# Hybrid attention block, out projection prepared on another schedule: sums of m later, loads on SP by an account, wo in 256 KB pieces, tail additions reordered

## The chip, the cores and the metric

One core of a Trainium2 chip runs the kernel. Its engines run their own instruction streams beside one another and meet by semaphores: TensorE (PE, matmuls; PEld are its weight loads), VectorE (DVE), ScalarE (ACT), GpSimd (POOL) and SyncE (SP), which here issues nearly all DMA transfers. An engine takes its instructions in order, and so does SP: a transfer that must wait holds up all that is queued behind it. The metric is the device time of one execution in microseconds (us), the median of the runs; 477.0 before the change.

## What is computed

One layer for 1024 tokens of width 1024: projections of x, two attention groups, gates, an out projection, a residual and a layer norm. All of it is float32.

```python
def reference(x, w_in, rel_pos_bias, sink_logits, w_out, ln_gain, ln_bias):
    h = jnp.einsum('bsd,de->bse', x, w_in[layer])
    q_a, k_a, v_a, z_a, q_b, k_b, v_b, z_b = jnp.split(h, SPLIT_POINTS, axis=-1)
    y_a = neighborhood_attention(q_a, k_a, v_a, rel_pos_bias)   # 8 heads of 64, 2-D window
    qb, kb = rotary(q_b, positions), rotary(k_b, positions)
    y_b = windowed_gqa_with_sink(qb, kb, v_b, sink_logits)      # 8 heads, |i - j| <= 128
    mixed = jnp.concatenate([y_a * jax.nn.silu(z_a), y_b * jax.nn.silu(z_b)], axis=-1)
    y = jnp.einsum('bse,ed->bsd', mixed, w_out[layer])
    x = layer_norm(DEEPNORM_ALPHA * x + y, ln_gain[layer], ln_bias[layer])
```

(The reshapes into heads are left out.) This change touches the last two lines and the preparation for them.

## The kernel before

**Number format.** A float32 operand is split into two float16 parts, hi (ACT: a scaled copy) and lo (DVE or POOL: the operand minus hi), and a product is three matmuls, hi by hi, hi by lo and lo by hi. On DVE such a lo is one instruction (L996 for wo, L1085 for m); on POOL it is two for wo (L998 and L999) and one for m.

**The stages.** Up to about 122 us come the projection of V and the first six of 21 projections of x. Then a loop of 138 steps runs 128 attention units, of group b first, then of group a. A unit is 128 queries of one head pair: scores (`stage_qk`, L851 and L852), bias and row maximum on DVE (L861), exp on ACT (L876), the split of the probabilities (ACT L886, DVE L887), a DMA transpose by SP (L890, tile `tr`), and, for four units together, the product with V (`stage_pv`, L916), the division (L925, L928), a transpose on TensorE (L939) and the gate, which writes the tile z of the transposed mixed matrix m (L942, L945). A transpose is used some steps after its unit's scores. Between the units `pump` and `pump_to` hand TensorE matmuls of the other 15 projections (L421) and, at the end, first products of the out projection (`out_head`). After step 137 `final()` does the rest of it.

**The out projection.** Features are grouped into four pairs of tiles of m. For the pairs 0 and 1 (group b) it goes by a scheme with seven products for eight, with sums of quarters: of m, S1 to S4 (A11, A12, A21, A22 are the quarters, cut by tile of the pair and half of the tokens), and of wo, T1 to T4 (B11 to B22 the quarters). The pairs 2 and 3 are multiplied plainly. The products are called q1, q2, q5, q6, q7, q3, p4 and d (the dictionary `TERMS`); several of them gather in one PSUM bank, and between them DVE adds what the bank holds to the output row block xr (`add`, L1181), so that the next product of a bank has to wait for the add ahead of it. For row blocks t and 4 + t the results come from the same products. When a block is whole, DVE takes its statistics (L1187, L1191), and ACT, POOL and SP do the norm and the store.

**What prepares it during the loop.** wo is loaded once to be scanned for a scale (`wo_load` L976, `wo_scan`; `wo_scale` with the small matmul L775), block 1 a second time for the sums T, whose parts go to DRAM (`td`, L1013) and come back at the end as tiles T0 to T3 (`t_soon`, L1030). The other parts of wo come in 14 loads `wob0` to `wob13` of 256 KB (`b_load` L1052), each into a staging buffer that an earlier one's split has freed: `wob5` reuses that of `wob0`, and so on. `b_split` queues a part's hi (L1061) and lo, `m_queue` the sums and splits of m. Row blocks of x are read by `x_soon` (L1040, scaled on ACT L1044) and in `final()` (`x_load` L1173, `x_scale` L1176).

**What sets the order.** Tables of step numbers by hand: SCAN_LD, M_AT, B_LD, B_AT, T_RD and X_RD say in which step an operation is queued. A queue per engine then gives them out: `pop` takes an operation when those it depends on were given out in earlier steps (for SP two or more steps earlier), `fill_in` one that fits into the gap that an account shows (`due`, time booked on an engine by estimated costs, against `at_step`, when a step is expected to begin). An operation of the kind "any" goes to ACT, DVE or POOL, whichever the account gives first. `need` pulls an operation forward when its result is about to be read. All this happens while the program is built; on the chip the order is fixed.

Of the kernel before, what the change touches and what calls it, by code (L numbers as in the profile page):

```python
# [7 lines left out]
F32 = mybir.dt.float32  # L8
# [36 lines left out]
SCAN_LD = [1, 8, 16, 24]  # L45
SCAN = (2, 3, 1, 0)
M_AT = [58, 67, 75, 83, 91, 99, 107]
B_KEYS = [("B11", 0), ("B21", 0), ("B11", 1), ("B21", 1), ("B22", 0), ("B22", 1), ("B11", 2), ("B21", 2),
          ("B11", 3), ("B21", 3), ("B12", 2), ("B22", 2), ("B12", 3), ("B22", 3)]
B_LD = [58, 59, 60, 61, 62, 69, 71, 73, 76, 80, 92, 94, 96, 98]  # L50
B_AT = [68, 70, 72, 74, 78, 80, 89, 91, 93, 95, 110, 112, 114, 116]
# [13 lines left out]
def hybrid_block(ctx, tc, xT, x, wt, wv, wo, bias, sink, gain, lbias, cos, sin, bmask, out):  # L65
# [84 lines left out]
    class Op:  # L150
        def __init__(self, eng, fn, deps, prio, cost=None):
            self.eng, self.fn, self.deps, self.step = eng, fn, [d for d in deps if d is not None], None
            self.cost = cost or WORK.get(eng, 0)
            self.prio, self.born, self.lag, self.fin = prio, clock["step"], 2 if eng == "sp" else 0, 0.0

# [43 lines left out]
    def fill_in(eng):  # L199
        now = at_step(clock["step"])  # L200
        ready = [op for e in (eng, "any") for op in queues[e] if op.prio > 1 and (e == eng or eng in op.cost) and all(
            d.step is not None and d.step + d.lag < clock["step"] + (d.eng == eng) and (d.eng == eng or d.fin < now)
# [761 lines left out]
    SUM, LOW = {"dve": 0.65, "pool": 1.2}, {"dve": 0.65, "pool": 1.85}  # L964
# [6 lines left out]
    wor, scans, t_ops = {}, [], []  # L971

    def wo_load(i, *deps):
        def load():
# [3 lines left out]
        load_ops["wor", i] = enq("sp", load, *deps)  # L978
        load_ops["wor", i].lag = 4

    def wo_scan(i):
        def scan(eng, b):
            m = wom[:, 4 * i + b:4 * i + b + 1]
            if eng == "act":
                nc.scalar.activation(junk2, wor[i][:, b], AF.Abs, accum_out=m)
            else:
                nc.vector.tensor_reduce(m, wor[i][:, b], axis=mybir.AxisListType.X, op=ALU.add,
                                        apply_absolute_value=True)

        for b in range(4):  # L990
            scans.append(enq("any", lambda eng, b=b: scan(eng, b), load_ops["wor", i], prio=1.9,
                             cost={"act": 0.85, "dve": 0.68}))
# [468 lines left out]
```

## Time and profile before

| | us |
|---|---|
| median of three runs (475.72, 477.00, 477.08) | 477.0 |
| the profiled execution | 477.5 |
| its span | 475.6 |
| scores of unit 64 (step 64) begin | 244.32 |
| scores of unit 96 begin | 311.53 |
| scores of unit 127, the last, begin | 378.99 |
| first product of `final()` (q5 of block 0) | 395.51 |
| mean granted clock of TensorE | 0.982 |

How to read the lines that follow below. In the first section of the page each engine has its busy time, its share of the span and its number of instructions. A line of the waits reads: engine, tile and line that waited, what it waited for, then us in total, times, and the longest. A line of the windows has a stretch of the span, its length, busy time and number of instructions of PE, PEld, DVE, ACT and POOL, then the granted clock (1.00 is full speed), the busy share of the DMA engines by packet time (it can pass 1), and GB/s. In a timeline, each row is start, duration, engine, line, operation, tiles out and in, the number of instructions merged, and in brackets the idle time ahead and what ended it. "SPq" is SP's queue: a long row is a transfer whose issue waited. Durations are of one profiled execution.

### The profile page before, as it was taken

The page shows a single profiled execution, that of the slowest core. Times are in us where ns is not written, and L with a number is a line of the kernel's source. Part 1 is how long each engine was busy: PE and PEld are TensorE (multiplying, and loading weights), DVE is VectorE, ACT ScalarE, POOL GpSimd, SP SyncE. Part 2 cuts the span into 40 slices and gives each one's busy share as a digit, 9 for nine tenths or more (in the row PEclk, how much of TensorE's full clock was granted, in tenths as well). Part 3 has the DMA queues.
Part 4 walks back from the last instruction along what each step waited for, and adds up shares of the span by engine and source line. Part 5 has one row for each costly group of instructions (what it writes and reads, how often), then busy time and mean ns, then how long its engine had stood idle before and what let it go on. Part 6 is the DMA issues. An engine that isn't in the chain of part 4 may idle for free.

```text
span 475.6 us, 9303 instructions
## 1 busy us (share of the span) xinstructions
PE 442.4 (93%) x3205; PEld 253.3 (53%) x3205; DVE 339.0 (71%) x826; ACT 313.6 (66%) x658; POOL 275.8 (58%) x292
## 2 busy tenths in 40 slices
PE   9999999999999999899979999959999969898993
PEld 8997744444455555455545555435555644343443
DVE  6979958069887888886887778775778734556554
ACT  5859689494797897868777777775788733133211
POOL 0300345648477388898287798984986331357551
PEclk9999999999999999999998999998999999999998
DMA  8911779951489995456999779569587698011122
GB/s 283 405 44 50 258 218 285 261 202 42 161 209 172 221 200 110 94 101 96 168 263 211 133 171 173 134 117 224 144 143 183 139 297 335 20 68 68 44 78 78
DMA packets 125791, 78.54 MB, mean 165 GB/s; under 512 B 96944, under 2 KB 106032, under 8 KB 125104
## 3 DMA queue, kind: packets, MB, share of 16 engines
q1 hardware_dynamic: 125600, 77.82, 66.2%
q8 instruction: 25, 0.41, 0.3%
q14 instruction: 22, 0.18, 0.1%
q10 hardware_dynamic: 144, 0.13, 0.1%
HBM read 46.44 MB, written 8.42 MB: 115 GB/s over the span
## 4 chain that ended last, share of the span: by engine, by line
PE 59%; DVE 10%; ACT 9%; issue 9%; DMA 6%; POOL 6%; SPq 0%; DVEq 0%; ACTq 0%; POOLq 0%
PE ps_pj L421 22%; PE ps_s L1146 9%; PE ps_s L528 6%; PE ps_pj L1146 5%; PE ps_t L916 4%; DMA tr<-split 3%; PE ps_pj L528 3%; PE ps_t L528 3%; ACT split L886 3%; PE ps_s L851 2%; PE ps_s L852 2%; PE ps_t L1146 2%; POOL wl L239 2%; DVE split L887 2%; DVE qs L297 2%
## 5 line engine op out<-in xcount | busy, mean ns | idle before, releaser
L421 PE MATMUL ps_pj<-xf,wh 128*128 128x512 f16 x672 | 203.8, 383 | 0.3 <-DVE qs L297 0.3
L421 PE MATMUL ps_pj<-xf,wl 128*128 128x512 f16 x336 | 128.7, 383 | 0.0
L887 DVE SCALAR_TENSOR_TENSOR split<-ps_s,split 128x384 f16<-128x384 f32 (+1 forms) x128 | 66.8, 522 | 44.3 <-ACT split L886 43.1
L421 PEld LDWEIGHTS <-wh 128*128 128x128 f16 x672 | 64.1, 99 | 63.0 <-issue 3.6
L876 ACT ACTIVATE ps_s<-sn,nm 128x385 f32<-128x385 f32 (+3 forms) x128 | 70.8, 553 | 28.8 <-DVE nm L861 28.5
L886 ACT ACTIVATE split<-ps_s 128x384 f16<-128x384 f32 (+1 forms) x128 | 58.3, 456 | 3.0 <-DMA tr<-split 1.3
L238 POOL TENSOR_SCALAR wr<-wr,wsc 128x512 f32<-128x512 f32 x26 | 20.5, 790 | 68.2 <-ACT wh L233 52.7
L421 PEld LDWEIGHTS <-wl 128*128 128x128 f16 x336 | 33.1, 99 | 39.1 <-issue 1.6
L916 PEld LDWEIGHTS <-tr 128*128 128x128 f16 (+1 forms) x1056 | 37.2, 98 | 14.5 <-DMA tr<-split 12.1
L851 PE MATMUL ps_s<-ks,qs 128*128 128x384 f16 (+2 forms) x128 | 40.0, 313 | 4.2 <-DVE split L887 3.4
L861 DVE CUSTOM_DVE_ANT_0 sn<-ps_s,bias,sg 128x368 f32<-128x368 f32 (+1 forms) x64 | 36.3, 567 | 9.1 <-PE ps_s L852 7.8
L861 DVE CUSTOM_DVE_ANT_0 sn<-ps_s,bm,nsk 128x384 f32<-128x384 f32 (+1 forms) x64 | 40.7, 636 | 1.2 <-PE ps_s L852 1.0
L852 PE MATMUL ps_s<-ks,qs 128*128 128x384 f16 (+2 forms) x128 | 40.0, 313 | 0.0
L1146 PEld LDWEIGHTS <-m 128*128 128x128 f16 x234 | 22.4, 99 | 30.6 <-issue 8.2
L239 POOL TENSOR_TENSOR wl<-wr,wh 128x512 f16<-128x512 f32 x26 | 32.7, 1256 | 2.2
L1193 ACT ACTIVATE sd<-mv,eps 128x1 f32<-128x1 f32 x8 | 2.4, 294 | 41.7 <-DVE mv L1191 41.7
L916 PE MATMUL ps_t<-va,tr 128*128 128x65 f16 (+1 forms) x528 | 20.7, 195 | 8.3 <-DMA tr<-split 8.3
L339 POOL COPY ks<-ks 64x512 f16<-64x512 f16 x40 | 26.0, 662 | 3.9 <-DVE ks L299 1.2
L1181 DVE SCALAR_TENSOR_TENSOR xr<-ps_s,yc,xr 128x512 f32<-128x512 f32 (+1 forms) x22 | 15.7, 729 | 15.8 <-PE ps_s L1146 15.8
L1146 PE MATMUL ps_s<-T,m 128*128 128x512 f16 x84 | 20.4, 379 | 5.1 <-DVE xr L1181 5.1
L1085 POOL TENSOR_TENSOR m<-z,m 128x512 f16<-128x512 f32 x15 | 17.1, 1162 | 13.7 <-ACT m L1082 13.6
L1242 POOL TENSOR_TENSOR xr<-xr,gb 128x512 f32<-128x512 f32 x13 | 16.5, 1271 | 13.2 <-ACT xr L1240 8.1
(208 smaller groups left out, 906.1 us busy)
## 6 DMA issues: line engine op xcount, KB each, us to landing
ws<-in_wt SPq DMA_DIRECT2D x15, 512.0 KB, 6.8
wr<-in_wt SPq DMA_DIRECT2D x26, 256.0 KB, 3.9
wor<-in_wo SPq DMA_DIRECT2D x5, 1024.0 KB, 5.7
xr<-in_x SPq DMA_DIRECT2D x8, 512.0 KB, 6.4
out<-xr SPq DMA_DIRECT2D x15, 256.0 KB, 2.0
wob<-in_wo SPq DMA_DIRECT2D x14, 256.0 KB, 4.1
bias<-in_bias SPq DMA_DIRECT2D x8, 440.0 KB, 4.0
wvraw<-in_wv SPq DMA_DIRECT2D x9, 320.0 KB, 5.6
```

The source lines that it names most:

```text
L239: nc.gpsimd.tensor_sub(l, raw, h)
L339: nc.gpsimd.tensor_copy(place(t, o, half, col), place(t, a, half, col))
L421: nc.tensor.matmul(ps, a[:, k % 4, :], mv, start=(k == 0 and i == 0), stop=(k == KT - 1 and i == 2))
L528: nc.tensor.matmul(ps[:, :320], lh[:, ts], rh[:, cs], start=(k == ko[0] and i == 0), stop=(k == ko[-1] and i == 2))
L851: nc.tensor.matmul(ps[:, :n], q, sl[0], start=True, stop=False)
L852: nc.tensor.matmul(ps[:, :n], q, sl[1], start=False, stop=True)
L861: nc.vector.tensor_tensor_reduce(sn[:, :n], ps[:, :n], bias_t, sg[:, c:c + 1], init, op0=ALU.add, op1=ALU.min, accum_out=nm)
L876: nc.scalar.activation(pt[:, :m], sn[:, :m], AF.Exp, bias=nm, scale=-1.0, accum_out=acc)
L886: nc.scalar.activation(hl[:, :m, 0, :], src, AF.Copy, scale=PSCALE)
L887: nc.vector.scalar_tensor_tensor(hl[:, :m, 1, :], src, PSCALE, hl[:, :m, 0, :], op0=ALU.mult, op1=ALU.subtract)
L916: nc.tensor.matmul(ps[:, w * m:w * m + e], a, b_, start=(i == 0), stop=(i == len(mms) - 1))
L1146: nc.tensor.matmul(ps[:, cs], lh[:, 128 * t:128 * t + 128], rh[:, cs], start=(fresh and e == 0 and n == 0), stop=(e == len(terms) - 1 and ...
```

## The change

- **wo for the scan** comes in 16 loads of 256 KB, one in every second step from 1 to 31, into one buffer of four slots, instead of four loads of 1 MB; the second reading of block 1 in four loads instead of one. A scan waits only for its own piece.
- **The scale of wo** is computed from step 38 on, when the account shows three units of time (`op.fin + 3`) after the last scan.
- **SP's loads** are given out only when the account shows that what they depend on has ended one unit of time before the step (`d.fin + 1.0 < at_step`).
- **m**: A11, A12 and A22 of the pairs 0 and 1 are split at steps 74 to 87, the sums S with their splits are queued from step 104 on (M_AT, M_KEYS).
- **wob** loads and splits have other steps and another order (B_LD, B_AT, B_KEYS), other homes for some tiles, and fewer dependencies. The account's costs for DVE's sums and lo parts go from 0.65 to 1.0.
- **x and T** are queued together at step 129, and an x block can be scaled on DVE too; four blocks become five in `final()`'s pool.
- **The tail**: the adds of q1's banks (`add(n, 0, b[n])`) for blocks 1 and 2 move forward into the rounds of blocks 0 and 1; p4 stands before q3; the norm of a block is divided in `begin` (statistics) and `finish` (the rest).

```diff
-SCAN_LD = [1, 8, 16, 24]
+SCAN_LD = range(1, 33, 2)
-M_AT = [58, 67, 75, 83, 91, 99, 107]
-B_LD = [58, 59, 60, 61, 62, 69, 71, 73, 76, 80, 92, 94, 96, 98]
+M_AT = [74, 80, 87, 104, 112, 119, 123]
+M_KEYS = (("A11", 0), ("A12", 0)), (("A11", 1), ("A12", 1)), (("A22", 0), ("A22", 1)), (("S3", 0), ("S1", 0)), \
+    (("S2", 0), ("S4", 0)), (("S3", 1), ("S1", 1)), (("S2", 1), ("S4", 1))
+B_LD = [62, 64, 66, 70, 72, 82, 84, 86, 92, 97, 104, 108, 111, 113]
+T_GO = 38
-T_RD = [124, 126, 128, 130]
-X_RD = [125, 127, 129, 131]
-ROOM = {"act": 0.5, "dve": 0.5, "pool": 0.0}
+ROOM = {"act": 0.2, "dve": 0.5, "pool": 0.0}
...
         ready = [op for op in q if op.prio <= top and all(
-            d.step is not None and d.step + d.lag < clock["step"] + (same and op.prio == 0 and d.eng == "act") for d in op.deps)]
+            d.step is not None and d.step + d.lag < clock["step"] + (same and op.prio == 0 and d.eng == "act")
+            and (eng != "sp" or d.fin + 1.0 < at_step(clock["step"])) for d in op.deps)]
...
-    SUM, LOW = {"dve": 0.65, "pool": 1.2}, {"dve": 0.65, "pool": 1.85}
+    SUM, LOW = {"dve": 1.0, "pool": 1.2}, {"dve": 1.0, "pool": 1.85}
...
-            wor[i] = rawp.tile([128, 4, 512], F32, tag="raw", name=f"wor{i}")
-            nc.sync.dma_start(wor[i], wo[i])
+        load_ops["wor", i, b] = enq("sp", lambda: nc.sync.dma_start(wor[:, b], wo[i, :, b]), *deps)
...
-        enq("act", lambda: nc.scalar.activation(xr_[t], xr_[t], AF.Copy, scale=ALPHA), load_ops["x", t], prio=1.7, cost=1.1)
+        enq("any", scale, enq("sp", load), prio=1.7, cost={"act": 1.1, "dve": 1.0}).wait = 4
...
-        for t in (2, 6, 3, 7):
+        for t in (5, 2, 6, 3, 7):
             x_load(t)
...
+        add(0, 0, b[0])
         for t in range(4):
-            if t == 3:
-                b[3] = run("q1", 3, bank("s"))
-            add(t, 0, b[t])
             cb = run("q5", t, bank("t" if t < 2 else "s"))
             run("q6", t, b[t])
             add(4 + t, 1, cb)
+            add(t, 1, b[t])
             if t == 3:
                 add(t, 1, cb)
-            add(t, 1, b[t])
-            if t < 3:
-                run("q2", t, a[t], (5,))
-                add(t, 0, a[t], whole=True)
+            finish()
+            for n in ((0, 1), (2,), (), ())[t]:
+                if n:
+                    add(n, 0, b[n])
+                run("q2", n, a[n], (5,))
+                add(n, 0, a[n], whole=True)
...
             add(4 + t, 1, b[t], whole=True)
-            if t < 3:
-                run("q3", t, cb)
-                add(t, 1, cb, whole=True)
-                norm(t)
+            if t == 2:
+                b[3] = run("q1", 3, bank("s"))
+                add(3, 0, b[3])
             run("p4", t, b[t])
             add(4 + t, 0, b[t], whole=True)
-            norm(4 + t)
+            if t == 3:
+                norm(7)
+            else:
+                begin(4 + t)
+                run("q3", t, cb)
+                add(t, 1, cb, whole=True)
+                finish()
+                begin(t)
...
-        if scans and len(scans) == 16 and all(op.step is not None and op.fin < at_step(i) for op in scans):
+        if i >= T_GO and len(scans) == 16 and all(op.step is not None and op.fin + 3 < at_step(i) for op in scans):
...
+        if i == 129:
+            x_soon(0)
+            t_soon(0)
+            t_soon(3)
+            x_soon(4)
+            x_soon(1)
+            t_soon(1)
+            t_soon(2)
```

The diff says little of where things land. On SP, the loads `wob5` to `wob9` before, in the steps 87 to 94 (`tr` are the units' transposes, `bias` the table of a group-a head):

```order
L1052 DMA wob5_4166<-in_wo 128x512
L890 DMA_TRANSPOSE tr_4175<-split2_1134 128x6x128
L890 DMA_TRANSPOSE tr_4194<-split3_1135 128x4x128
L823 DMA bias_4207<-in_bias 128x880
L1052 DMA wob6_4209<-in_wo 128x512
L890 DMA_TRANSPOSE tr_4258<-split4_1136 128x4x128
L1052 DMA wob7_4271<-in_wo 128x512
L890 DMA_TRANSPOSE tr_4280<-split5_1137 128x6x128
L1052 DMA wob8_4302<-in_wo 128x512
```

and after, in the steps 96 to 100 (`va2` holds the values of a head pair):

```order
L795 DMA va2_4400<-vd_75 128x8x260
L893 DMA_TRANSPOSE tr_4425<-split4_1136 128x6x128
L1051 DMA wob5_4439<-in_wo 128x512
L893 DMA_TRANSPOSE tr_4448<-split5_1137 128x4x128
L826 DMA bias_4461<-in_bias 128x880
L1051 DMA wob6_4464<-in_wo 128x512
L893 DMA_TRANSPOSE tr_4507<-split0_1132 128x4x128
L1051 DMA wob7_4519<-in_wo 128x512
L893 DMA_TRANSPOSE tr_4528<-split1_1133 128x6x128
L1051 DMA wob8_4544<-in_wo 128x512
```

The five loads moved some seven steps back and stand one in each step; the lo parts that free their buffers are on POOL.

SP at the end of the loop before, from the transpose of unit 124 on:

```order
L890 DMA_TRANSPOSE tr_5382<-split4_1136 128x6x128
L1030 DMA T0_5391<-td_76 128x2x1024
L890 DMA_TRANSPOSE tr_5400<-split5_1137 128x6x128
L1040 DMA xr4_5413<-in_x 128x1024
L890 DMA_TRANSPOSE tr_5422<-split0_1132 128x6x128
L1030 DMA T1_5430<-td_76 128x2x1024
L890 DMA_TRANSPOSE tr_5434<-split1_1133 128x4x128
L1040 DMA xr1_5446<-in_x 128x1024
```

and after:

```order
L893 DMA_TRANSPOSE tr_5414<-split0_1132 128x6x128
L893 DMA_TRANSPOSE tr_5425<-split1_1133 128x4x128
L1035 DMA xr0_5436<-in_x 128x1024
L1025 DMA T0_5438<-td_76 128x2x1024
L1025 DMA T3_5440<-td_76 128x2x1024
L1035 DMA xr4_5448<-in_x 128x1024
L1035 DMA xr1_5450<-in_x 128x1024
L1025 DMA T1_5452<-td_76 128x2x1024
```

All loads of x and T now follow the last unit's transpose.

On DVE at the same place, the last gate (`z3`) and the first adds of `final()`, before:

```order
L928 TENSOR_TENSOR on_5404<-ps_t_5519,ri_5557 128x4x64
L945 SCALAR_TENSOR_TENSOR z3_5106<-ps_t_5569,zc_101,z3_5106 128x16x32
L1167 MEMSET eps_5579 128x1
L1181 SCALAR_TENSOR_TENSOR xr0_5339<-ps_s_5499,yc_108,xr0_5339 128x512
L1181 SCALAR_TENSOR_TENSOR xr4_5413<-ps_t_5598,yc_108,xr4_5413 128x512
```

and after:

```order
L931 TENSOR_TENSOR on_5397<-ps_t_5517,ri_5557 128x4x64
L1041 TENSOR_SCALAR xr1_5450<-xr1_5450 128x1024
L948 SCALAR_TENSOR_TENSOR z3_5102<-ps_t_5573,zc_101,z3_5102 128x16x32
L1172 MEMSET eps_5584 128x1
L1091 TENSOR_TENSOR A12_3_5596<-z3_5102,A12_3_5596 128x512
L1186 SCALAR_TENSOR_TENSOR xr0_5436<-ps_s_5497,yc_108,xr0_5436 128x512
L1186 SCALAR_TENSOR_TENSOR xr4_5448<-ps_t_5607,yc_108,xr4_5448 128x512
```

The scaling of xr1, the fifth of the loads above, and the lo of A12 of pair 3 now stand ahead of the first add.

More of the change, by code (lines that the diff above doesn't have):

```diff
@@ L201, in fill_in @@
         ready = [op for e in (eng, "any") for op in queues[e] if op.prio > 1 and (e == eng or eng in op.cost) and all(
-            d.step is not None and d.step + d.lag < clock["step"] + (d.eng == eng) and (d.eng == eng or d.fin < now)
+            d.step is not None and d.step + max(d.lag, op.wait) < clock["step"] + (d.eng == eng) and (d.eng == eng or d.fin < now)
             for d in op.deps)]
@@ L1293, in m_last @@
     def m_last():
-        r7 = big_home["r7"]
-        pair_of(r7, ("A12", 3), ("A22", 3))
+        for n in ("A12", "A22"):
+            t = tiles["kq"].tile([128, 2, 512], F16, tag="ks", name=f"{n}_3", bufs=8)
+            part[n, 3] = t[:, 0], t[:, 1]
         z = zt[ZP[3][1]]
```

102 lines of the change are left out of this document (53 added, 49 removed).

## The prediction

> **What bounds the kernel now.** I read the page's busy times first, then TensorE's waits over the whole span, then the granted clock in the stretches where those waits lie, and last what each waited-for engine or queue was doing.
>
> ```profile
> PE 442.4 (93%) x3205; PEld 253.3 (53%) x3205; DVE 339.0 (71%) x826; ACT 313.6 (66%) x658; POOL 275.8 (58%) x292
> ...
> PE ps_t L916 <- DMA tr<-split: 11.0, 8, 3.3
> PE ps_s L1146 <- DVE xr L1181: 5.1, 5, 1.8
> PE ps_s L851 <- DVE split L887: 3.4, 4, 0.9
> PE ps_t L775 <- DVE z L942: 2.2, 1, 2.2
> ...
> 180.00:200.00 20.00, 17.78 (x167) 10.27 (x165) 17.30 (x54) 15.65 (x42) 16.24 (x19) 1.00 0.44 86
> 240.00:260.00 20.00, 17.17 (x133) 9.07 (x132) 15.83 (x44) 14.53 (x33) 15.94 (x17) 0.91 1.15 237
> 300.00:320.00 20.00, 13.26 (x106) 6.89 (x105) 15.05 (x39) 14.74 (x30) 16.89 (x20) 0.97 0.63 130
> 320.00:340.00 20.00, 20.00 (x161) 11.18 (x160) 13.34 (x34) 13.15 (x26) 13.18 (x16) 0.86 0.82 178
> 380.00:400.00 20.00, 15.40 (x123) 8.19 (x121) 7.60 (x17) 9.21 (x13) 6.26 (x6) 0.91 1.10 343
> ```
>
> TensorE works 93% of the span, and both kernels give it the same matmuls in the same order up to the last unit. So the change can only pay by taking away TensorE's waits, and what follows them: the clock column after busy (1.00 elsewhere) drops to 0.91, 0.86 and 0.91 just after the three worst groups of waits. A clock of 0.91 over 20 us is 1.8 us of lost matmul time; 0.97 and 0.86 in two rows are 0.6 + 2.8 = 3.4. The waits on transposes (11.0 us) are the largest group; three stretches hold them:
>
> ```profile
> PE ps_t L916 <- DMA tr<-split: 2.7, 3, 1.0
> ...
> PE ps_t L916 <- DMA tr<-split: 4.6, 2, 3.3
> ...
> PE ps_t L916 <- DMA tr<-split: 3.7, 3, 1.7
> ```
>
> These are the answers for 240-260, 300-325 and 380-400.
>
> **The change, part by part.** *1. SP's stand at 303-313 goes: 8.0 us.* The transposes are issued by SP, in order with the loads:
>
> ```profile
> 303.10 0.41 SPq L1052 DMA_DIRECT2D wob<-in_wo  x1
> 303.61 1.19 SPq L890 DMA_TRANSPOSE tr<-split  x1
> 313.15 0.33 SPq L1052 DMA_DIRECT2D wob<-in_wo  x1
> ...
> 311.39 1.69 DVE L996 SCALAR_TENSOR_TENSOR wo<-wob,wsn,wo 128x512 f16<-128x512 f32 x1
> ...
> SPq L1052 <- DVE wo L996: 8.3, 1, 8.3
> SPq L1052 <- POOL wo L999: 4.5, 2, 2.3
> ...
> 244.32 0.27 PE L851 MATMUL ps_s<-ks,qs 128*128 128x256 f16 x1
> ...
> 311.53 0.27 PE L851 MATMUL ps_s<-ks,qs 128*128 128x256 f16 x1
> ```
>
> For 8.3 us the queue stood at one 256 KB load, whose buffer DVE freed only with the lo part at 311.39 + 1.69; the next transpose was queued behind it, and TensorE then waited 4.6 us and lost 3.4 by the clock. After, that load stands at steps 96 to 100, three steps behind the POOL operation that frees its buffer; steps 64 and 96 began at 244.3 and 311.5, so a step is 2.1 us and three are 6.3. Gain 4.6 + 3.4 = 8.0 us; nothing if POOL is as late as DVE was (a rival).
>
> *2. The cluster at steps 58 to 63 is spread: 4.5 us.* A 1 MB load of wo, five 256 KB ones and two of bias lie between 236 and 256; transposes took 5.5 us to land there, against 3.3 in the median of all 128.
>
> ```profile
> tr<-split SPq DMA_TRANSPOSE x9, 5.5
> ...
> tr<-split SPq DMA_TRANSPOSE x128, 3.3
> ```
>
> After, these nine loads of 256 KB lie in 13 steps. The waits of 2.7 us and the 1.8 of clock go. Bounds: a half of it may stay, 2.2.
>
> The 1 MB loads become 20 of 256 KB. The Trainium skill, "DMA: Bandwidth & Descriptors", section Bandwidth, speaks against that: it says to batch to 1 MiB or more, and gives about 2 us fixed plus the bytes at 436 GB/s; by it the same bytes would take 20 x 2.6 = 52 us instead of 5 x 4.4 = 22, an estimate. I cost it at nothing, since the DMA share in 180:200 above is 0.44 and TensorE waits for no transpose there.
>
> *3. The scale of wo (L775) a step later: 1.9 us.*
>
> ```profile
> 192.02 0.68 DVE L987 TENSOR_REDUCE wom<-wor 128x1 f32<-128x512 f32 x1
> 193.21 0.75 DVE L942 SCALAR_TENSOR_TENSOR z<-ps_t,zc,z 128x512 f32<-128x512 f32 x1
> ```
>
> TensorE's small matmul was at the head of its queue while DVE still had the last scan and more in front. The account now asks for three more units of time after the last scan, and six projection matmuls stand before it. Of 2.2 us I take 1.9, with 0.3 left.
>
> *4. More work on DVE in the loop: -2.0 us.* DVE gets four scans of wo instead of seven (0.68 each, as above: 2.0 us less), but two sums of T (none), two lo parts of m (one) and four lo parts of wo (three), so four more operations with two SBUF inputs. The trace has one such lo alone at 0.74 us and one beside POOL at 1.69:
>
> ```profile
> 382.44 0.74 DVE L996 SCALAR_TENSOR_TENSOR wo<-wob,wsn,wo 128x512 f16<-128x512 f32 x1
> ...
> 314.13 0.32 PE L851 MATMUL ps_s<-ks,qs 128*128 128x368 f16 x1 [0.93 <-DVE split L887]
> ```
>
> Behind the slow one the next split came late and TensorE waited 0.93. Four more cost between 0 (they fall into DVE's idle time; it is busy 71% of the span) and 4 x 0.93 = 3.7; I take 2.0, nearly the middle, since the fewer scans speak for the low end and POOL's share of 16 to 17 of 20 us for the slow row. The Trainium skill, "SBUF — State Buffer", section "SBUF: two separate sides", says why: DVE with two SBUF inputs and GpSimd share a port pair, and the later one blocks fully. The two rows of L996 agree.
>
> *5. A new cluster at steps 96 to 101: -1.0 us.* Five loads of wo, one of va (520 KB) and one of bias (440 KB), 2.2 MB in five steps. It is like the stretch of part 2, and about as dense: 2.2 MB in five steps of 2.1 us are 210 GB/s beside the transposes, against 237 with them in 240:260 above; but it lasts half as long, and no single load is over 520 KB. Bounds 0 and the 4.5 of part 2; I take 1.0, nearer to nothing.
>
> *6. The start of the tail: -2.4 us.* Before, the loads of T and x lie between the last transposes, whose 3.7 us of waits and 1.8 of clock (380:400) would seem to be won, since all of them now follow the last transpose. But others wait for them. The rows from the last scores (378.99, called P) on:
>
> ```profile
> 378.99 0.27 PE L851 MATMUL ps_s<-ks,qs 128*128 128x256 f16 x1
> 395.51 1.46 PE L1146 MATMUL ps_t<-T,m 128*128 128x512 f16 x6
> 397.19 1.46 PE L1146 MATMUL ps_s<-T,m 128*128 128x512 f16 x6 [0.22 <-DVE xr L1181]
> ...
> 382.09 0.42 DVE L887 SCALAR_TENSOR_TENSOR split<-ps_s,split 128x256 f16<-128x256 f32 x1 [0.72 <-ACT split L886]
> ...
> 384.27 1.06 ACT L1044 ACTIVATE xr<-xr 128x1024 f32<-128x1024 f32 x1 [1.59 <-DMA xr<-in_x]
> ...
> DMA to landing us min/median/max: 4.2/5.7/6.4
> ...
> DMA packets 7860, 8.66 MB, mean 309 GB/s; under 512 B 5563, under 2 KB 5563, under 8 KB 7856
> ```
>
> q6 of tile 0 started at P + 18.2. Without the waits and the slow clock TensorE would be there 5.7 us earlier, at P + 12.5. After, the last split is ready at P + 3.5, its transpose holds SP for 1.2, and the loads go out from P + 4.7: xr0, T0, T3, xr4, xr1. The first lands 4.2 later (the least that a T load took), each further 512 KB after 1.3 to 1.7 (1.7 at the mean 309 GB/s of this stretch, 1.3 at its best slices of about 400): xr1 at P + 14.1 to 15.7. DVE has the scaling of xr1 in front of the last z, so behind it come, one after the other, that scaling (not in the trace on DVE; ACT's 1.06), z 0.75, ACT's copy of z 0.56, the lo of A12 0.75, and the add that frees q6's bank 0.75, 3.9 us in all. q6 starts between P + 18.0 and P + 19.6, say P + 18.8: 0.6 later than before. TensorE has then stood some 6 us, and the 1.8 of slow clock, which before lay ahead of q6, comes behind it: 2.4 lost. Bounds: 4 gained if xr1 lands by P + 10, before z is ready; 4 more lost if the seven loads share the queues evenly (7 x 1.7 + 2.5 after P + 4.7).
>
> *7. The order of the tail: +1.5 us.*
>
> ```profile
> 400.15 2.10 PE L1146 MATMUL ps_pj<-wo,A 128*128 128x512 f16 x9 [0.85 <-DVE xr L1181]
> 414.95 1.45 PE L1146 MATMUL ps_s<-T,m 128*128 128x512 f16 x6 [1.70 <-DVE xr L1181]
> 431.83 0.38 PE L1146 MATMUL ps_s<-T,m 128*128 128x512 f16 x1 [1.82 <-DVE xr L1181]
> 448.72 1.46 PE L1146 MATMUL ps_s<-T,m 128*128 128x512 f16 x6 [0.55 <-DVE xr L1181]
> 454.90 1.45 PE L1146 MATMUL ps_s<-T,m 128*128 128x512 f16 x6 [0.84 <-DVE xr L1181]
> ...
> 400.13 0.69 DVE L1187 BATCH_NORM_STATS2 stats<-xr 128x6 f32<-128x512 f32 x1
> ```
>
> The adds of tiles 1 and 2 move forward, into tile 0 and 1, which takes away the 1.70, 1.82 and 0.55, and about half of the 0.85 at d (its bank is freed earlier in DVE's queue): 4.5 us. p4 now follows q7 directly in tiles 0 and 1, as it did in tile 3 (the 0.84): 1.7 us; in tile 2, q1 of tile 3 stands between. And q3 of tile 0 waits for the lo of S4, which DVE does behind an add, statistics and their sum: 0.75 + 0.69 + 0.23 + its own 0.75 is 2.4 us after p4, against 1.1 us of q3's first five matmuls, so 1.3. That is 4.5 - 1.7 - 1.3 = 1.5 us gained; 0.1 if the statistics that now stand ahead of adds cost 0.69 twice, 2.8 if the lo of S4 is early.
>
> **Sum.** 8.0 + 4.5 + 1.9 - 2.0 - 1.0 - 2.4 + 1.5 = 10.5 us off the profiled span of 475.6, so 465.1. That execution took 477.5, 1.9 more than its span, and 0.5 more than the median of the runs shown, 477.0: 465.1 + 1.9 - 0.5 = **466.5 us**.
>
> **Rivals.** *A, the tail's start is won as well.* xr1 lands by P + 10 and q6 goes some 4 us earlier, without the slow clock (part 6 at +4 instead of -2.4): 466.5 - 6.4 = 460. For it: no transpose shares the queues with the loads any more; against: a T load took up to 6.4 us, and five loads stand in a row. *B, the loop gives back more.* Parts 4 and 5 at their upper bounds, 3.7 + 4.5 instead of 3.0: 466.5 + 5.2 = 471.7. For it: DVE at 17.30 of 20 us in 180:200; against: SP's order shows the new cluster as the lighter one. *C, slower than before: POOL is the late one.* wob5 to wob9 each wait for a lo on POOL, and each stands ahead of transposes. If POOL is more than 6.3 us late at two of these five loads, SP stands twice: the 8.0 of part 1 are lost and 8.0 more paid, 466.5 + 16 = 482.5. For it: SP stood 4.5 us for POOL at two such loads before, and POOL is the busiest of the helpers in 300:320 (16.89); against: those two were of 2.3 us at most. With one such stand it is *D, the change does not do what it says*: 466.5 + 8 = 474.5. *E, the small scan loads crowd the transposes* in steps 1 to 31: a group of waits like the 2.7 of part 2 in each of four blocks, 10.8 us, which ends at 477. For it: the rows of 5.5 against 3.3 us show that loads do delay transposes; against: the DMA share of 0.44 at 180:200. The rule on batches that part 2 cites from "DMA: Bandwidth & Descriptors" of the Trainium skill would make this case likelier; no wait in the trace bears it out so far.
>
> **How the numbers follow.** Forecast 0.48 (its own range 462 to 471), A 0.17, B 0.15, C 0.11, D 0.05, E 0.04. The range 457 to 475 holds the forecast, B, D and most of A, and leaves out C, E and the far end of A, 0.19 in all. A time within 0.3% of 477.0 (475.6 to 478.4) could not be told from no change. Faster: forecast, A, B and D, less 0.02 for their upper ends, 0.83; same: E and 0.01 of D, 0.05; slower: C and 0.01 of B's end, 0.12.
>
> **What would show it.** Right: no wait on a transpose over 1 us between steps 60 and 110, SP's loads of wob never waiting over 2.5 us, the clock near 1.00 in 240 to 340, step 127's scores some 11 us earlier than 378.99; then one gap of about 6 us before q6 of tile 0, ended by DVE and behind it the load of xr1. Wrong: the last scores less than 7 us earlier (B, C or D: the waits on splits, or SP's waits on POOL, tell which), or q6 less than 16 us behind them (A).

## The result and the profile after

The changed kernel takes 471.0 us (median of four runs, 470.86 to 471.55) beside 476.36 for the kernel before (475.41 to 477.08): a ratio of 0.9891, interval 0.9868 to 0.9914, so 5.4 us or 1.1% faster. The forecast was 466.5 us, with a range of 457 to 475. The profiled execution took 470.95, its span is 468.8.

The page's busy times and the waits of TensorE over the whole span, after:

```profile
PE 440.1 (94%) x3205; PEld 250.7 (53%) x3205; DVE 340.4 (73%) x828; ACT 314.6 (67%) x663; POOL 271.5 (58%) x287
...
PE ps_s L1151 <- DVE xr L1186: 9.8, 4, 7.2
PE ps_s L854 <- DVE split L890: 5.2, 8, 1.6
...
PE ps_t L1151 <- DVE m L1091: 1.3, 1, 1.3
...
PE ps_t L919 <- DMA tr<-split: 1.0, 2, 0.5
...
PE ps_t L778 <- DVE z L945: 0.2, 1, 0.2
```

The wait on transposes fell from 11.0 to 1.0 us and the one at the scale from 2.2 to 0.2. Two others grew: the additions of the tail from 5.1 to 9.8, with one gap of 7.2 among them, and the splits in the loop from 3.4 to 5.2. The same stretches as before in the windows (clock behind the five busy times):

```profile
240.00:260.00 20.00, 19.50 (x164) 10.88 (x160) 16.64 (x47) 15.33 (x35) 9.67 (x13) 1.00 1.03 203
300.00:320.00 20.00, 17.91 (x143) 9.33 (x143) 15.89 (x42) 15.58 (x31) 14.05 (x17) 1.00 0.82 170
320.00:340.00 20.00, 18.31 (x177) 10.29 (x174) 15.98 (x41) 16.17 (x32) 15.23 (x17) 1.00 0.91 193
380.00:400.00 20.00, 12.38 (x48) 5.13 (x46) 8.51 (x14) 7.67 (x9) 3.91 (x4) 0.74 0.88 341
```

The slow clock is gone from the loop, and has grown from 0.91 to 0.74 in the one stretch where the tail starts. Of the loads `wob`, none waits on SP for over 0.6 us any more; before, one waited 8.3.

But for the small one of the scale, TensorE gets the same matmuls in the same order in the loop, so the progress of the two kernels can be laid side by side. These are the times from the scores of one unit to those of the fourth after it, read from the two timelines, where they differ by over 0.3 us (neighbouring rows are joined):

| units | before | after | difference |
|---|---|---|---|
| 32 to 36 | 7.34 | 7.98 | +0.65 |
| 36 to 40 | 10.19 | 8.19 | -2.01 |
| 48 to 52 | 8.16 | 9.76 | +1.60 |
| 60 to 68 | 20.23 | 15.61 | -4.62 |
| 80 to 92 | 23.39 | 25.76 | +2.36 |
| 92 to 100 | 25.28 | 16.99 | -8.29 |
| 100 to 112 | 24.05 | 26.56 | +2.51 |
| all, unit 0 to 127 | 256.67 | 249.04 | -7.63 |

The three waits that were to go went, and 14.9 us with them. But 7.1 us came back in four other places, three of them some units behind a gain. (The first, 0.65 at units 32 to 36, is a wait of 0.47 on a transpose.)

These are figures of one execution each, and some of them change from one execution to the next although the order of instructions there is the same. Units 32 to 40 take 15.7 to 17.3 us in e1, e2, e3 and e7 below, where the changed kernel's profile has 16.2 and that before 17.5. Units 60 to 68 take 18.0 in e8 and 18.8 in e12, where the profile before has 20.2.

How the 1.60 looks, on ACT after:

```profile
214.47 1.26 ACT L296 CAST qs<-rp_raw 64x512 f16<-64x512 f32 x2 [1.74 <-POOL rp_raw L362]
215.75 0.49 ACT L889 ACTIVATE split<-ps_s 128x384 f16<-128x384 f32 x1
```

ACT stood 1.74 us for a rotary product of POOL, copied it twice, and only then made the split whose bank TensorE's next scores were waiting for (1.64 us). Before the change ACT stood there for the same 1.74 us; TensorE was later by 1.4 us then and lost only 0.66.

The start of the tail, TensorE, DVE and ACT in turn, last scores at 371.31:

```profile
382.79 1.47 PE L1151 MATMUL ps_t<-T,m 128*128 128x512 f16 x6 [0.39 <-DMA T<-td]
391.49 2.72 PE L1151 MATMUL ps_s<-T,m 128*128 128x512 f16 x6 [7.23 <-DVE xr L1186]
394.00 5.38 PE L1151 MATMUL ps_pj<-wo,A 128*128 128x512 f16 x18
399.22 1.03 PE L1151 MATMUL ps_s<-T,m 128*128 128x512 f16 x4
...
388.04 0.69 DVE L1041 TENSOR_SCALAR xr<-xr 128x1024 f32<-128x1024 f32 x1 [7.78 <-DMA xr<-in_x]
388.65 0.75 DVE L948 SCALAR_TENSOR_TENSOR z<-ps_t,zc,z 128x512 f32<-128x512 f32 x1
...
386.80 1.06 ACT L1039 ACTIVATE xr<-xr 128x1024 f32<-128x1024 f32 x1 [4.96 <-DMA xr<-in_x]
387.76 1.12 ACT L1088 CAST m<-z 128x512 f16<-128x512 f32 x2
```

DVE stood 7.78 us for the load of xr1 and ACT 4.96 for that of xr4, each with the work for q6 queued behind. q6 starts 20.2 us after the last scores, against 18.2 before, and its first 24 matmuls take 7.7 us where 24 at full clock take 5.2.

### The profile page after: what moved, and what is told of

The parts are those of the page before. It is cut to its first block, busy times and chain, and to the rows that moved or that the text cites. A ratio compares the mean times of both kernels' runs of the same rounds, so it can differ in the third digit from the quotient of the medians.

```text
span 468.8 us, 9315 instructions
## 1 busy us (share of the span) xinstructions
PE 440.1 (94%) x3205; PEld 250.7 (53%) x3205; DVE 340.4 (73%) x828; ACT 314.6 (67%) x663; POOL 271.5 (58%) x287
## 4 chain that ended last, share of the span: by engine, by line
PE 38%; DVE 22%; ACT 16%; issue 11%; POOL 6%; DMA 5%; SPq 1%; DVEq 0%; ACTq 0%; POOLq 0%
PE ps_s L1151 9%; PE ps_pj L424 7%; PE ps_s L531 5%; PE ps_pj L1151 5%; ACT split L889 5%; DVE split L890 3%; ACT ps_s L879 3%; PE ps_pj L531 3%; PE ps_t L531 3%; ACT wh L236 3%; DVE sn L864 3%; DVE qs L300 2%; DVE ks L300 2%; PE ps_t L1151 2%; DMA xr<-in_x 2%
## 5 line engine op out<-in xcount | busy, mean ns | idle before, releaser
L424 PE MATMUL ps_pj<-xf,wh 128*128 128x512 f16 x672 | 201.3, 379 | 2.3 <-DVE qs L300 1.5
L424 PE MATMUL ps_pj<-xf,wl 128*128 128x512 f16 x336 | 127.3, 379 | 0.0
L424 PEld LDWEIGHTS <-wh 128*128 128x128 f16 x672 | 63.0, 98 | 64.2 <-DVE qs L300 2.8
L1151 PEld LDWEIGHTS <-m 128*128 128x128 f16 x180 | 17.1, 99 | 31.6 <-issue 10.3
L1151 PEld LDWEIGHTS <-A 128*128 128x128 f16 x216 | 20.5, 99 | 21.9 <-issue 2.2
L342 POOL COPY ks<-ks 64x512 f16<-64x512 f16 x40 | 27.0, 685 | 5.2 <-DVE sn L861 1.3
L1254 ACT ACTIVATE xr<-xr,nmr,rstd 128x1024 f32<-128x1024 f32 x6 | 7.4, 1240 | 28.6 <-POOL nmr L1205 28.6
L855 PEld LDWEIGHTS <-qs 128*128 128x128 f16 x128 | 12.5, 98 | 23.3 <-issue 10.5
L241 POOL TENSOR_SCALAR ws<-ws,wsc 128x512 f32<-128x512 f32 x16 | 11.1, 695 | 23.0 <-ACT wh L236 10.9
## 6 DMA issues: line engine op xcount, KB each, us to landing
xr<-in_x SPq DMA_DIRECT2D x8, 512.0 KB, 10.2
```

The source lines that it names most:

```text
L241: nc.gpsimd.tensor_scalar(raw, raw, scale, 1.0, op0=ALU.mult, op1=ALU.mult)
L424: nc.tensor.matmul(ps, a[:, k % 4, :], mv, start=(k == 0 and i == 0), stop=(k == KT - 1 and i == 2))
L855: nc.tensor.matmul(ps[:, :n], q, sl[1], start=False, stop=True)
L1151: nc.tensor.matmul(ps[:, cs], lh[:, 128 * t:128 * t + 128], rh[:, cs], start=(fresh and e == 0 and n == 0), stop=(e == len(terms) - 1 and ...
```

## The experiments

Each kernel ran beside the kernel before the change on the same chip; ratios are to that one. Two questions had to be settled: what holds q6 up, and why half of the loop's gain came back.

**e1, xr1's scaling out of DVE's queue** (of the changed kernel).

```diff
-        enq("any", scale, enq("sp", load), ...).wait = 4
+        ld = enq("sp", load)
+        if t != 1:
+            enq("any", scale, ld, ...).wait = 4
...
         m_last()
+        x_scale(1)
```

> The changed kernel, but the scaling of xr1 is no longer in DVE's queue ahead of the last gate z; ACT does it behind its copies of z. Question: is the 7.23 us gap before q6 of block 0 due to that one load alone? Theory one (xr1 in DVE's queue is the only gate): the gap falls to under 1 us, and with the slow clock behind it some 9 us go, 462 us. Theory two (a second chain of the same length runs through ACT: the load of xr4, its scaling until 387.9, the copies for S2 and S4, the copies of z): q6 starts only some 0.6 us earlier, the gap stays at 6 to 7 us, and the time is 470 to 471 us. I hold theory two.

470.32 us, 0.9847 (0.9793 to 0.9901). The gap is 6.50 instead of 7.23:

```profile
391.67 1.87 PE L1153 MATMUL ps_s<-T,m 128*128 128x512 f16 x4 [6.50 <-DVE xr L1188]
...
387.62 1.06 ACT L1039 ACTIVATE xr<-xr 128x1024 f32<-128x1024 f32 x1 [5.42 <-DMA xr<-in_x]
388.58 1.12 ACT L1090 CAST m<-z 128x512 f16<-128x512 f32 x2
389.61 1.13 ACT L1090 CAST A<-z 128x512 f16<-128x512 f32 x2
```

With xr1 gone from DVE, the chain through ACT ends the same wait, as theory two had it: xr4's load, its scaling, four copies. The forecast's part 6 had named only the first chain.

**e2, both chains freed.** xr4 and xr1 are scaled on ACT behind all the copies, and the add for q6 comes first.

```diff
+        if t == 0:
+            enq("act", lambda: scale("act"), ld, ...)
...
+        need(*done["S2", 1], *done["S4", 1])
+        add(0, 0, obank["q1", 0])
         m_last()
+        x_scale(4)
+        x_scale(1)
...
-        add(0, 0, b[0])
```

> The changed kernel, with the scalings of xr4 and xr1 on ACT behind the copies for S2, S4 and z, and the add that frees q6's bank ahead of the last parts of A12 and A22. Theory one (the gap is a wait on the loads of xr4 and xr1 that sit in front of work which doesn't need them): the gap before q6 falls from 7.23 us to under 1.5 us, the granted clock in 380:400 goes back above 0.95, and the time is 461 to 464 us. Rival (the loads of T, or d and q7 waiting for the add of xr4 behind its load, bind next): the gap moves behind q6 and 4 us or more of it stay, 466 to 469 us.

462.73 us, 0.9688 (0.9626 to 0.9751). Theory one holds:

```profile
385.25 1.47 PE L1153 MATMUL ps_t<-T,m 128*128 128x512 f16 x6 [1.36 <-DMA T<-td]
386.86 1.47 PE L1153 MATMUL ps_s<-T,m 128*128 128x512 f16 x6
...
391.29 2.75 PE L1153 MATMUL ps_pj<-wo,A 128*128 128x512 f16 x12 [1.34 <-DVE xr L1188]
...
380.00:400.00 20.00, 16.16 (x103) 7.52 (x101) 10.51 (x17) 9.16 (x11) 6.69 (x6) 1.00 0.94 364
```

q6 follows q5 with no wait on an add, two waits of 1.4 us stand in place of 7.23, and the clock stays at 1.00. From the last scores to the end of the span it is 89.2 us, against 97.5 in the changed kernel and 96.7 before. The two scalings and the add were moved together, so how the gain divides between them isn't shown.

**e3, the loads of T and x between the last transposes again**, as before the change.

```diff
-        if i == 129:
-            x_soon(0)
-            t_soon(0)
...
+        if i in (124, 126, 128, 130):
+            t_soon((3, 0, 1, 2)[(i - 124) // 2])
+        if i in (125, 127, 129):
+            x_soon((0, 4, 1)[(i - 125) // 2])
```

> The changed kernel, with the loads of T and x queued one by one in the steps 124 to 130, between the last transposes, as before the change. Theory one (the new place of the loads only trades one wait for another): waits on transposes behind the last scores come back with 2.5 to 4.5 us, the wait before q6 falls under 2 us, and the time is within 1.5 us of the changed kernel's 471.0. Rival (the old place is clearly better): 467 us or less. Second rival (clearly worse, the transposes wait more than before): 473 us or more.

467.45 us, 0.9782 (0.9717 to 0.9846). The waits came as forecast, 4.5 us on transposes and 1.6 before q6, but the sum is better than the changed kernel by more than the 1.5 us allowed, 0.5 above the first rival's bound of 467:

```profile
PE ps_t L919 <- DMA tr<-split: 4.5, 3, 2.1
PE ps_s L1151 <- DVE xr L1186: 1.6, 1, 1.6
...
380.00:400.00 20.00, 14.33 (x75) 6.73 (x76) 8.22 (x14) 7.97 (x10) 5.42 (x5) 0.83 0.86 307
```

Moving the loads was thus no even trade: 6.1 us of waits in four pieces against 7.6 in two (7.23 and 0.39), and the clock 0.83 against 0.74. From the last scores to the end it is 94.9 us against 97.5: the new place of these loads cost the change 2.6 us in these two executions.

**e4, the sums T of wo later.**

```diff
             wo_scale()
             scans.clear()
-            t_prep(0)
+            tp["at"] = 54
+        if i == tp.get("at"):
+            t_prep(0)
```

> The changed kernel, with the sums and splits T of wo queued from step 54 on instead of right behind the scale at step 39. Question: why does the 2.0 us gained at the scale shrink by 1.6 us between units 48 and 52? Theory one (POOL is full there and ACT stands 1.74 us for its rotary products; one sum of T on POOL, 1.3 us, stands ahead of them): units 48 to 52 take 8.2 to 8.6 us instead of 9.76. Rival (POOL's own projections and rotary work set the time there in any case): 9.5 us or more. The whole time is not forecast closely, since later loads of wo move too: 469 to 474 us.

462.99 us, 0.9694 (0.9636 to 0.9753), far better than forecast. Units 48 to 52 take 7.34, less than theory one gave. ACT there:

```profile
213.96 0.62 ACT L296 CAST qs<-rp_raw 64x512 f16<-64x512 f32 x1 [1.65 <-POOL rp_raw L362]
214.48 0.48 ACT L889 ACTIVATE split<-ps_s 128x384 f16<-128x384 f32 x1
```

Counted from the scores of unit 48 (212.05 here, 210.87 in the changed kernel), POOL's product is 1.7 us earlier, and one copy of 0.6 us instead of two stands before the split. So POOL's load is the larger part of it, and ACT's order the smaller. The medians are 8.0 us apart; the two profiled spans, which the rest goes by, 6.5. Of these only 0.9 are won up to the last scores (at 370.40), though the loop from unit 0 on is 1.9 shorter: this execution reached unit 0 1.0 later. The other 5.6 are the tail: here both lo parts for A12 and A22 fell to POOL, so that the add for q6 no longer stands behind one of them, another 2.18 us of wait fell ahead of q5, and the wait before q6 is 1.92, with the clock at 0.92. From the last scores to the end it is 91.9 us. That agrees with e2 that the time lies in this place.

**e5, e2 and e4 together.**

> e2 and e4 together: the scalings of xr4 and xr1 out of the way, the add for q6 early, and the sums T of wo from step 54 on. e2's time from the last scores to the end (89.2 us of span) behind e4's loop (last scores at 370.4) would be a span of 459.6. Theory one (the two act at different places and add up, but for the 2.2 us that DVE's late sums of m cost behind the last scores in e4): 460 to 462 us. Rival (e4 already had most of e2's gain, since its copies of z no longer stand ahead of the add): no better than either, 462.5 to 464 us.

462.12 us, 0.9672 (0.9612 to 0.9733; runs from 459.28 to 464.02). This lies between the two forecasts, and its runs overlap those of e2 and of e4, so it doesn't tell. Last scores at 369.93, end 90.8 later.

**e6, the changed kernel without the rule for SP's loads.**

```diff
-            d.step is not None and d.step + d.lag < clock["step"] + (same and op.prio == 0 and d.eng == "act")
-            and (eng != "sp" or d.fin + 1.0 < at_step(clock["step"])) for d in op.deps)]
+            d.step is not None and d.step + d.lag < clock["step"] + (same and op.prio == 0 and d.eng == "act") for d in op.deps)]
```

> The changed kernel without the rule that SP takes a load only when the account shows its buffer free; the loads wob5 to wob8 then stand at the transposes of units 85 to 90 again, as before the change. Theory one (the rule is what keeps SP from standing): SP stands 3 us or more at one of these loads, TensorE waits 2 us or more for transposes in the units 84 to 100, and the time is 473 to 478 us. Rival (the lo parts that free the buffers are early enough now, the rule is idle): no wait of SP at wob over 2.5 us, time 470 to 472 us.

473.29 us, 0.9905 (0.9872 to 0.9937). SP stands again, and again for a lo part that DVE does late:

```profile
SPq L1050 <- DVE wo L991: 2.9, 1, 2.9
SPq L1050 <- POOL wo L994: 1.9, 2, 1.6
...
315.07 0.68 PE L918 MATMUL ps_t<-va,tr 128*128 128x65 f16 x9 [3.46 <-DMA tr<-split]
```

So the rule is not idle, though the longest stand of 2.9 us is just short of theory one's 3. Units 96 to 100 take 12.93 us against 8.68 with it; but units 104 to 112 then take 16.2 instead of 18.5, so that of 4.3 us some 2 come back. (The loads stand earlier here, and four hi and lo parts of wo have left the units 103 to 106 with them, so not all of this need be TensorE's stand.) What the rule is worth in the whole time isn't shown: this ratio and the changed kernel's 0.9891 lie within each other's intervals.

**e7, the changed kernel with wo's lo parts on POOL.**

```diff
-... o, prio=1.8, cost=LOW)
+... o, prio=1.8, cost={"pool": 1.85} if n < 10 else LOW)
```

> The changed kernel with the lo parts of wob0 to wob9 on POOL only, so that three of them leave DVE (one in each of the units 88 to 110). Theory one (part 4 of the prediction: lo parts on DVE delay the splits and the projections' additions): the units 104 to 112 lose at least 1.4 of their 2.3 us against before, and the time falls to 468 to 470 us. Rival (ACT's extra copies are late, or POOL becomes the late one): those units stay within 0.5 us of 18.5 us in all, time 470.5 to 474 us.

468.79 us, 0.9821 (0.9782 to 0.986). The time lies in theory one's range, but the units 104 to 112 gained only 0.6 of the 1.4 us or more (0.9 in units 100 to 112). The account put a sum of m on DVE at unit 106, where a lo part had been, and the largest wait there (1.27 us, on a projection's addition) is unchanged to 0.01. So it isn't the lo parts that make this wait; they are at most a part of the 2.5 us.

**e8, the kernel before with one part: wob5 to wob9 later.**

```diff
-B_LD = [58, 59, 60, 61, 62, 69, 71, 73, 76, 80, 92, 94, 96, 98]
-B_AT = [68, 70, 72, 74, 78, 80, 89, 91, 93, 95, 110, 112, 114, 116]
+B_LD = [58, 59, 60, 61, 62, 93, 94, 95, 96, 97, 103, 105, 107, 109]
+B_AT = [68, 70, 72, 74, 78, 97, 99, 100, 102, 104, 112, 114, 116, 117]
```

> The kernel before the change, with one part alone: the loads wob5 to wob9 and their splits stand some six steps later (transposes of units 91 to 96), all else as before. Theory one (part 1 of the prediction, SP's stand at wob7 is worth 8.0 us by itself): no SP wait of over 3 us at these loads, units 96 to 100 take 8 to 9 us instead of 16.3, and the time is 467 to 470 us. Rival (the time is lost elsewhere, since DVE's lo part of wo4 stays as late and the later splits crowd the last steps): 472 us or more.

469.05 us, 0.9831 (0.9791 to 0.9872): 8.4 us below the kernel before on the same chip, and no slower than the whole change. Theory one holds: no load `wob` waits over 0.5 us, units 96 to 100 take 7.97. Units 92 to 100 are 9.1 us shorter, units 100 to 112 take 26.2 instead of 24.05.

**e9, the kernel before with one part: the scale of wo later.**

```diff
-        if scans and len(scans) == 16 and all(op.step is not None and op.fin < at_step(i) for op in scans):
+        if i >= 38 and len(scans) == 16 and all(op.step is not None and op.fin + 3 < at_step(i) for op in scans):
```

> The kernel before the change with one part alone: the scale of wo is computed from step 38 on, three units of the account's time after the last scan (with the sums T of wo behind it by as much). Theory one (a wait that is removed is mostly given back where ACT and POOL are the next late ones): units 36 to 40 take 8.0 to 8.4 us instead of 10.19, units 48 to 52 take 9.4 to 9.8 instead of 8.16, and of the 2 us at most 0.7 are left at unit 64, so the time is the same within its interval. Rival (part 3 of the prediction: the 1.9 us stay): units 48 to 52 within 0.3 us of 8.16, unit 64 begins 1.7 us or more earlier.

475.9 us, 0.9976 (0.9944 to 1.0009): the same. Units 36 to 40 take 8.59, a little over theory one's range, units 48 to 52 9.39 and 52 to 56 8.78 instead of 8.30: of 1.6 us gained nothing is left at unit 64. The sums T follow the scale, and the account now puts two of them on DVE instead of POOL; one (1.34 us, at 216.01) stands in unit 49, right behind the longer of the waits below. The wait moved from the scale to the splits:

```profile
PE ps_s L851 <- DVE split L887: 1.9, 2, 1.4
PE ps_s L851 <- DVE sn L856: 0.3, 1, 0.3
```

**e10, the kernel before with its 1 MB loads in four pieces.**

```diff
-            nc.sync.dma_start(wor[i], wo[i])
+            for b in range(4):
+                nc.sync.dma_start(wor[i][:, b], wo[i, :, b])
```

> The kernel before the change with one part alone: each 1 MB load of wo is issued as four of 256 KB in the same place, so that the bytes and their moment stay. Theory one (the crowd of loads at steps 56 to 62 delays the transposes, whatever the size of a piece): units 64 to 68 take 11 to 12.5 us as before (11.99), no change of the time beyond its interval. Rival (the single transfer of 1 MB is what blocks): units 64 to 68 fall below 9 us. Second rival (small pieces cost more, by a fixed part of each): waits on transposes grow by 1 us or more.

475.14 us, 0.9952 (0.9937 to 0.9966). Units 64 to 68 take 8.91, the waits on transposes there are 1.5 us instead of 2.7 and the clock stays at 1.00. That is the first rival's number, and theory one's 11 to 12.5 is missed, but it doesn't show that the size of the load is the cause: in e9, where the load was whole, the waits were 1.5 and the units 8.93 as well, with the clock at 1.00 too. The second rival, a price for each small piece, is out.

**e11, e5 with the lo parts on POOL.**

> e5 with the lo parts of wob0 to wob9 on POOL only, as in e7, as a version that may beat both kernels. e7's gain in units 100 to 112 was 0.9 us, so if it adds up: 460.5 to 462 us against 462.1 of e5. Rival (POOL, which has the late sums T too, becomes the late one): 462.5 to 466 us.

461.45 us, 0.9655 (0.9625 to 0.9686): the fastest median of all, 9.5 us below the changed kernel's, though its runs (460.01 to 462.87) overlap those of e2, e4 and e5. Units 100 to 112 take 26.8 as in e5, so the lo parts on POOL gain nothing there.

**e12, the kernel before with one operation on another engine.**

```diff
-... o, prio=1.8, cost=LOW)
+... o, prio=1.8, cost={"pool":1.85} if n == 4 else LOW)
```

> The kernel before the change, with one operation on another engine: the lo part of wo4, for which SP stood 8.3 us, goes to POOL right behind that of wo3; ACT's and SP's orders stay, nothing is put into the units 100 to 112. Question: do those units lose 2.5 us in the changed kernel because of work that was added there, or because TensorE, no longer held up before them, runs into helpers that were covered by the stand? Theory one (covered helpers): SP stands under 3 us, units 96 to 100 take 8 to 9.5 us instead of 16.34, and units 100 to 112 take 25.5 to 26.6 instead of 24.05; time 468 to 471 us. Rival (added work): units 100 to 112 stay within 0.5 us of 24.05, time 467 to 469 us. If SP still stands 5 us or more, POOL is as late as DVE was and the run doesn't tell.

471.21 us, 0.9886 (0.9805 to 0.9967): as fast as the whole change, within a wide interval (one run took 475.81). The median is 0.2 above theory one's range; its other numbers hold: SP waits at most 2.2 us at these loads, units 96 to 100 take 8.06, and units 100 to 112 take 26.60, where nothing was put. (In return for the lo of wo4 the account gave DVE one lo of m, at unit 98; from unit 99 on ACT, DVE and POOL have the same order as before.)

```profile
SPq L1052 <- POOL wo L999: 4.5, 2, 2.2
...
PE ps_pj L421 <- DVE qs L297: 1.7, 1, 1.7
...
338.70 0.72 ACT L233 ACTIVATE wh<-ws,wsc 128x512 f16<-128x512 f32 x1
339.45 0.49 ACT L886 ACTIVATE split<-ps_s 128x384 f16<-128x384 f32 x1
```

The 1.7 us is the wait that the changed kernel has as 1.3 and the kernel before not at all: a weight's hi part on ACT ahead of a split, DVE's addition for the projection behind that split, TensorE behind the addition. Before, TensorE came there 8 us later and found it done.

How far the helpers are behind can be counted: ACT's split of unit 100 starts 3.8 us after the unit's scores before, and 7.1 in e12; that of unit 108 5.0 and 7.6. The stand of 8.3 us had let them come closer. The same run shows it at units 48 to 56 by chance: TensorE lost 1.7 us more than before at units 36 to 40 (11.86, by a drop of the clock behind the scale's wait), in the same order of instructions, and units 48 to 56 then took 15.11 instead of 16.46. It isn't always so: e1 and e2 took 1.1 us longer than the changed kernel at units 36 to 40, and units 48 to 52 took 9.7 and 9.8 all the same.

## Why the prediction was right, and where its sizes were off

The direction, the range and the likeliest case held: the loop gains, the tail's start gives back. By the forecast's own steps, in us gained:

| part | forecast | measured | from |
|---|---|---|---|
| 1, SP's stand | 8.0 | 8.3 | units 92 to 100; 9.1 there in e8 |
| 2, the cluster at 58 to 63 | 4.5 | 4.6 | units 60 to 68 |
| 3, the scale of wo | 1.9 | 2.0 | units 36 to 40 |
| 4 and 5, new waits in the loop | -3.0 | -7.1 | units 32 to 36, 48 to 52, 80 to 92, 100 to 112 |
| 6, the tail's start | -2.4 | -4.5 | q6 2.0 later, 2.5 of slow clock behind it |
| 7, the tail's order | 1.5 | 1.9 | waits after q6, 7.6 before and 5.7 after |

The parts come to 5.2 us, while the two profiled spans differ by 6.8 (and the medians by 5.4). The other 1.6 lie behind TensorE's last wait, where the last store took 3.6 us to land before and 2.3 after; they are in no part.

*Parts 1 to 3* were right in mechanism, and in size for these two executions. e8 and e12 remove the first wait singly, with 9.1 and 8.3 us at its place, and e9 the third, with 1.6. No run removes the second singly. That its 4.6 met the forecast of 4.5 is in part luck: with the same cluster in place, e8 and e12 lose only 2.4 and 3.2 us against the changed kernel's 15.6, since the waits and the drops of the clock there vary. Part 2's formula of 2 us plus the bytes stands in the Trainium skill, "DMA: Bandwidth & Descriptors", in the section "Anatomy of one DMA — SWDGE (gpsimd) path", where it is fitted to transfers that GpSimd issues; here SP issues them, and no run shows it.

*Part 4* is the term that failed, in size and in cause. It put the loop's losses down to four more operations of DVE beside POOL, at 0.93 us each at most. The runs show something else: TensorE's waits had let ACT, DVE and POOL catch up, and where a wait goes, the next place at which those three are late comes out. e12 is the clear case: the units 100 to 112 lost 2.5 us with no work added there. The scale's 1.6 us came back whole within 16 units in e9: ACT's split that TensorE waited for there started at 215.01, and at 216.07 before, so the helpers came out only 1.1 us earlier where TensorE was 1.8 earlier; but a sum of T had also moved beside it. So the price should have gone by the gains, about half of them here (7.1 of 14.9, in one pair of executions), not by added operations. That DVE is slowed beside POOL was true, but small in the loop: sums of T took 0.93 and 1.34 us, wo's lo parts 0.80 to 1.03, m's 0.89 and 1.55. The row of 0.74 that part 4 calls alone was not: POOL's next operation started 0.33 behind it and took 0.96 instead of 0.69, so there the later one paid. Its count left out two sums of m (0.84 and 0.68) that leave DVE in the loop. For the units 80 to 92 the evidence is weaker: e8, e9 and e10 all lose 1.4 to 2.3 us between units 76 and 88 after gaining 2.2 to 3.1 at 64, with nothing added there. But 0.8 of the changed kernel's 2.4 lie in units 88 to 92, where e8, e9, e10 and e12 take 8.2 as before; the changed kernel has copies and a lo of m moved there, and no run took those away alone.

*Part 5* cost nothing: no wait on a transpose is seen in units 92 to 104.

*Part 6* had the right place and one of its two chains. xr1 landed 16.7 us after the last scores, where 14.1 to 15.7 were forecast, the steps behind it took 3.5 us for 3.9, and the slow clock cost 2.5 for 1.8 (1.9 in e6 and e7, behind gaps of 6.3 and 6.2). e2 measures what the place is worth: 8.3 us from the last scores to the end.

*The rivals.* A (the tail's start won as well) did not come, but e2 shows what it would have given. B (the loop gives back more, 471.7) is what the number looks like, by another cause than B named. C and D (SP stands again) did not come; e6 shows them in small, without the rule. E did not come: up to unit 60 the only new wait on a transpose is one of 0.5 us, at 182, and of e1, e2, e3, e6 and e7 only e7 has it. The Trainium skill's rule on batches ("DMA: Bandwidth & Descriptors", section Bandwidth) would have spoken for E; e10 shows four pieces of 256 KB no slower than one transfer of 1 MB at this place.

**Still open:** how much of the 2.4 us at units 80 to 92 is work moved there; how the gain of e2 divides between the scalings and the add; how e4's 5.6 us in the tail come about; and what the cluster of part 2 costs in the middle of many executions.

## What to carry to other kernels

When one engine is nearly full and its helpers run at 75 to 85%, a wait that is removed is worth what it lasts only up to the next place where a helper is late; look for that place a few steps on, and count on part of the gain coming back. An in-order queue that carries both loads and the critical transfers must not meet a load whose buffer is still in use: one operation on another engine was worth 5 to 7 us here (e12, by the ratio and by the medians). And before work that the critical engine waits for, put nothing that waits for a load it doesn't need: with two scalings and the last parts of m out of the way of one add, the tail was 8.3 us shorter.

## What was not expected of the hardware

The granted clock drops on stops far shorter than expected, and not each time. A drop shows as a stretch at 0.50: 3.4 us long at 250.67 before, 6.8 at 318.94, and 10.2 at 386.45 in the changed kernel, so the shortest costs 1.7 us. Three waits of 0.87, 1.00 and 0.83 us within 3.6 us were followed by such a drop, 0.91 over the 20 us around (before), and so were two of 0.94 and 0.79 (e12); three of 0.38, 1.00 and 0.81 at the same place left it at 1.00 (e8), and so did two of 0.66 and 0.82 or of 0.68 and 0.83 (e10, e9). The single wait of 2.2 us at the scale left it at 1.00 before and came with 0.91 in e12, where units 36 to 40 then took 11.86 us instead of 10.19. Units 64 to 68 took 11.99 us before and 8.9 in e9 and e10: 1.2 us of waits less, 3.1 us of time. The Trainium skill, "TensorE: Matmul & The Clock Gate", section "HAM oscillation — how this bites in real kernels", gives as a rule no idle gaps over about 3.4 us; here two or three gaps of up to 1.0 us were enough in two executions and not in three others.

Twelve loads of 512 KB stand in a row behind the last transpose in the changed kernel, the seven of step 129 and five of `final()`. They land 1.2 to 2.8 us apart: the first 3.8 us after its issue, the seventh 10.2. Before, with transposes between them, the loads of T and x up to `final()` took 4.2 to 7.4.
